# Moving the sums of squares of a linear-attention output, and of the compressed queries, by stages

## The chip, the cores and the metric

The kernel runs on one core of one Trainium2 chip. The metric is device time in microseconds (us). Three runs of the kernel before took 2260.86, 2266.12 and 2268.09 us, so the median is 2266.12 us.

## What is computed

The reference is a three-layer model on 1024 tokens of width 1024. The first layer mixes a convolution, a pooling branch and a differential attention, and ends in a mixture of 16 experts. The change doesn't touch it. The other two layers (numbered 0 and 1 here) are of one form:

```
u = rmsnorm(h, ln_mix[i]) @ w_in[i]
(c_q, c_kv, k_rope, gate_a, gq, gk, gv, lr_f, lr_b, gate_g) = split_cols(u, IN_SPLITS)
y_mla = mla_branch(c_q, c_kv, k_rope, ...) * silu(gate_a)
y_gla = gla_branch(gq, gk, gv, lr_f, lr_b, ..., gla_out_norm[i]) * silu(gate_g)
h = h + concatenate([y_mla, y_gla]) @ w_out[i]
h = h + sigmoid(rmsnorm(h, ple_norm[i]) @ w_ple_gate[i]) * (p[i] @ w_ple_proj[i])
```

Two parts matter. The linear attention (gla_branch) has four heads. For each it computes, in chunks of 64 tokens and in both directions, o = intra-chunk part + (queries times a running state), then rmsnorm(o_forward + o_backward) over the head's 128 columns. The softmax attention (mla_branch) works on compressed queries c_q (384 columns) and compressed keys and values c_kv (256 columns): both are normalised by their root mean square, the queries and keys get a part that rope rotates, and scores, softmax and values follow. Dividing a row of queries by its root mean square is the same as scaling its scores, so the kernel multiplies the raw c_q by its weights and applies the factor 1/rms inside the softmax.

## The kernel before

All activations stand transposed (features on partitions, 1024 tokens along the free axis). A float32 product is made of three matmuls on a high and a low half of each operand: helper split (line 451 makes the high half on ScalarE, line 447 the low half on VectorE, or, every third time, on GpSimd). In the code the engines are nc.tensor (PE), nc.vector (DVE), nc.scalar (ACT), nc.gpsimd (POOL) and nc.sync (SP).

The order of the work is written by hand with Python generators. Each yield ends a stage. `_weave(main, side, steps)` takes a stage of main, then on average `steps` stages of side, and so on; `_chain` runs generators one after the other. The framework that compiles the program takes this order as a priority: an instruction that it expects to be late can be overtaken by others of its engine. It fixes one order per engine, and each engine then runs its list strictly in that order. Buffers come from pools by tag: PSUM has four product buffers of 512 columns (tag mm: psT, psSq and others) and two of 1024 columns (tag sc: psGt, psA, psK, psDS, psO, psS, psKR and the scores). A buffer is taken when its tile is first written and is free after its last reader.

`second_layer` (line 2001) weaves two things after the first eight half products of gla_v. The main side is a chain of products from the input projection (mmT and gla_v: a stage is half a product of 512 columns, 12 matmuls of 128x512; psT or psV). The other side is `gla_heads(i, 16)` (line 1735), which starts one of four `gla_head` generators every 16 of its stages and advances all that are alive, oldest first. The stages of one head (line 1623), counted from 0, before the change:

- 0: psGt, the gate's product (L1633), its read-out; 2 and 3: scans and exponentials; 4 and 5: scaling of queries qd and keys kd; 6: two more scalings (POOL writes L, L1666)
- 8 and 9: psA, intra-chunk products (L1678), each read by a masked copy into xbuf (L1679), then summed on POOL (L1682)
- 10: psK, transposes (L1689); 11: two memsets; 12: psDS, state increments (L1700), two buffers of tag sc
- 13 to 15: the state chain st, 30 small VectorE instructions (L1703, L1706)
- 18: psO, the output (L1717 and L1720, 8 x 6 matmul records of 128 and 64 columns), copied to go by ACT (L1722)
- 19: ms_split: psS is taken, ACT squares go (L589), the square is split (sqh, sql); 21: psS, a product with ones in four matmuls (L595: two on sqh, two on sql), which sums over partitions
- 22: gr = 1/rms by ACT's Ln (L598) and Exp (L599); 23: go times weight times gr on DVE (L1727), times the gate on POOL (L1730), store by SP (L1732)

Inside the chain, c_q's three products (mla_c, line 1745) are woven at 0.5 with `mla_norm` (line 1776), which takes another buffer of tag sc for the sums of squares of c_kv (psS at L1786, read by ACT at L1788), while heads 2 and 3 are alive. mla_c also adds up the squares of c_q in one tile css.

After the heads come the rope inputs (mla_rope_in, four stages of 9 matmuls), and then a weave of `mla_nope` (line 1833: eight query stages of 9 matmuls and eight key stages of 6; ACT reads each into a high half, qnh or knh, L1823, and DVE makes the low half, qnl or knl, L1824) with a chain of `rope` (line 1860) and `mla_factor` (line 1799), at 1.2. Rope has 15 stages: 1 loads tables (SP), 2 multiplies the key part, 6 takes psKR and splits it, 7 and 8 multiply on POOL, 9 to 12 rotate the queries on DVE (L1892 to L1898), 13 splits their first half into r1h and r1l, 14 the second into r2h and r2l, and 15 issues 16 SP copies into qr (L1907). mla_factor is a single stage: eight one-column products psSq of css with ones (L1805), each seen as two matmul records, then rq by ACT (L1809, L1810) and DVE (L1812). rq scales the softmax. The scores (L460, psS<-krh,qr among them) start next; each takes three matmuls on qn and kn and two on qr.

Of the kernel before, what the change touches and what calls it, by code (L numbers as in the profile page):

```python
# [19 lines left out]
NT = 8  # L20
# [242 lines left out]
def _weave(main, side, steps=1.0):  # L263

    due = 0.0
    for _ in main:
        yield
        due += steps
        while due >= 1.0:
            due -= 1.0  # L270
            if next(side, _END) is not _END:
                yield
    yield from side
# [10 lines left out]
def _chain(*gens):  # L284
    for g in gens:
        yield from g
# [31 lines left out]
class _Kernel:  # L318
# [261 lines left out]
        nc.scalar.activation(out, ps, AF.Ln, bias=self.eps, scale=1.0 / n)  # L580
        nc.scalar.activation(out, out, AF.Exp, scale=-0.5)

    def ms_split(self, srcs, n, out):

        nc = self.nc
        ps = self.sc("psS")
        for j, s in enumerate(srcs):
            q = self.d("sqs")
            nc.scalar.activation(q, s, AF.Square)  # L589
            parts = self.split(q, "sq")  # L590
            yield
            yield
            for m, part in enumerate(parts):
                for b in (slice(0, 512), slice(512, 1024)):
                    nc.tensor.matmul(ps[:, b], self.ones_r, part[:, b], start=j == 0 and m == 0,  # L595
                                     stop=j == len(srcs) - 1 and m == 1)
            yield
        nc.scalar.activation(out, ps, AF.Ln, bias=self.eps, scale=1.0 / n)  # L598
        nc.scalar.activation(out, out, AF.Exp, scale=-0.5)  # L599
# [1023 lines left out]
    def gla_head(self, i, h):  # L1623
# [48 lines left out]
        for q in range(2):  # L1672
            ps = self.sc("psA", (128, 2, 4, 128))
            for a in range(4):
                for dr in range(2):
                    r = slice(64 * dr, 64 * dr + 64)
# [20 lines left out]
        for t in range(8):  # L1697
            for e in range(2):
                r = slice(64 * e, 64 * e + 64)
                nc.tensor.matmul(ds[e][:, t], kn[r, t], v(t)[r], start=True, stop=True)  # L1700
        yield
        for c in range(15):
            nc.vector.scalar_tensor_tensor(st[(c + 1) // 8][0:64, (c + 1) % 8], st[c // 8][0:64, c % 8],  # L1703
                                           er[0:64, 1, c:c + 1], ds[c % 2][0:64, c // 2], op0=OP.mult, op1=OP.add)
            r = 15 - c
# [4 lines left out]
        yield  # L1710
        yield
        yield

        o = self.d("go")
        ps = self.sc("psO", (128, 8, 128))
# [6 lines left out]
        nc.scalar.activation(o, ps.rearrange("p a b -> p (a b)"), AF.Copy)  # L1722
        yield
        r = self.d("gr")
        yield from self.ms_split([o], 128, r)
        yield
        nc.vector.scalar_tensor_tensor(o, o, self.col(("go", i)), r, op0=OP.mult, op1=OP.mult)  # L1727
        while h not in self.sg:
# [70 lines left out]
    def mla_factor(self, i):  # L1799

        nc = self.nc
        css = self.css.pop("cq")
        pc = self.mm("psSq", (128, 8))
        for t in range(NT):
            nc.tensor.matmul(pc[:, t:t + 1], css[:, 128 * t:128 * t + 128], self.ones[:, 0:1],  # L1805
                             start=True, stop=True)
        rq = self.const.tile([128, 2, 8], F32, name="rq", tag="rq")
        self.rq = rq[:, 0], rq[:, 1]
        nc.scalar.activation(rq[:, 1], pc, AF.Ln, bias=self.eps, scale=1.0 / 384)  # L1809
        nc.scalar.activation(rq[:, 1], rq[:, 1], AF.Exp, scale=-0.5)  # L1810
        for n, f in enumerate((192.0 ** -0.5, -192.0 ** -0.5)):
            nc.vector.tensor_scalar(rq[:, n], rq[:, 1], f, None, op0=OP.mult)  # L1812
        yield
# [187 lines left out]
    def second_layer(self, i, lead):  # L2001
# [4 lines left out]
        heads = self.gla_heads(i, 16)  # L2006
# [4 lines left out]
            values, self.gla_gate(i, 1), self.gla_qk(i, 2), self.gla_qk(i, 3),  # L2011
            self.gla_gate(i, 2), self.gla_gate(i, 3), self.mla_gate(i, 0), self.mla_gate(i, 1), self.mla_c(i, "ckv"),
            _weave(self.mla_c(i, "cq"), self.mla_norm(i), 0.5), self.mla_gate(i, 2), self.mla_gate(i, 3)),
            heads, 1.06)
        self.hm = None
        self.ahead = 1
        yield from self.mla_rope_in(i)
        yield from _weave(self.mla_nope(i), _chain(self.rope(i), self.mla_factor(i)), 1.2)
        self.ahead = 0
        attention = self.mla_attention(i)  # L2020
        values = self.mla_values(i)
# [271 lines left out]
```

## Time and profile before

| what | value |
|---|---|
| median of three runs | 2266.12 us |
| the profiled execution | 2267.0 us |
| its span in the profile | 2265.2 us |
| PE busy | 2142.4 us (95%) |
| DVE, ACT, POOL busy | 66%, 51%, 22% |
| TensorE's granted clock, mean over the span | 0.978 |

The profile's times are microseconds from the start of the span. "Busy" adds up the engine's instructions; a matmul's end is modelled, and consecutive matmuls overlap. A wait is idle time of an engine just before an instruction, put down to the instruction that released it. The granted clock is a share of TensorE's full speed: 1.00 is 2.4 GHz, 0.50 is 1.2 GHz, and a value between them is a mean over a stretch with both. In a timeline line, the first number is the start, the second the duration of the group of like instructions, "x" counts them, and the square bracket holds the idle time before the first, and its releaser. PEld is the weight load of a matmul.

### The profile page before, as it was taken

Reading aid. Unit: us, or ns where it says so; the run is one execution under the profiler, and the core shown is the slowest. Engines: PE = TensorE matmul, PEld = TensorE weight load, DVE = VectorE, ACT = ScalarE, POOL = GpSimd, SP = SyncE. Lnnn points to the kernel's source line nnn. Section 1 sums busy time; section 2 is a strip of 40 time slices with the busy share of each in tenths; the row PEclk is TensorE's granted clock in tenths of the full one; section 3 lists DMA queues with packets and bytes.
Section 4 is the critical chain, followed back from the end, with each engine's and each line's share of the span. In section 5 each row is a group of like instructions: output and inputs, shape, how many; then the busy total and the mean of one; then the engine's idle time right before and its main releaser. Section 6 shows DMA issues by size and latency. Waiting matters only on the chain.

```text
span 2265.2 us, 31258 instructions
## 1 busy us (share of the span) xinstructions
PE 2142.4 (95%) x11660; PEld 1814.3 (80%) x11660; DVE 1498.1 (66%) x2598; ACT 1153.1 (51%) x2192; POOL 493.8 (22%) x431
## 2 busy tenths in 40 slices
PE   7989888998999989999999999999999989999998
PEld 7878777787887778877788988888877777898886
DVE  5995788577788732677746674566367675675455
ACT  5314778435677654354444553456344444554344
POOL 1320144202232101112322331101011232332100
PEclk9999999999999999999999999999999999999999
DMA  5101231638999861011112024543001113013343
GB/s 199 47 19 57 75 84 34 213 118 290 282 326 325 268 235 56 28 38 66 45 58 56 10 75 160 187 144 129 10 28 57 47 66 84 11 43 135 121 149 130
DMA packets 78447, 255.09 MB, mean 113 GB/s; under 512 B 9680, under 2 KB 16976, under 8 KB 78288
## 3 DMA queue, kind: packets, MB, share of 16 engines
q1 hardware_dynamic: 65024, 205.84, 26.1%
q0 software_dynamic: 10672, 38.00, 7.1%
q10 hardware_dynamic: 2592, 9.18, 1.1%
q8 instruction: 94, 1.54, 0.3%
q14 instruction: 65, 0.53, 0.1%
HBM read 183.51 MB, written 58.98 MB: 107 GB/s over the span
## 4 chain that ended last, share of the span: by engine, by line
PE 46%; DVE 10%; issue 3%; ACT 3%; DMA 1%; POOL 1%; SPq 0%; DVEq 0%; ACTq 0%; POOLq 0%
PE psR L501 14%; PE psT L470 11%; PE psS L460 6%; PE psO L460 4%; PE psV L501 4%; PE psPT L1951 2%; DVE st L1703 2%; DVE st L1706 2%; PE psMV L460 1%; PE psX L550 1%; DVE wl L447 1%; PE psA L1678 1%; DVE B L1648 1%; PE psO L1720 1%; DVE B L1647 1%
## 5 line engine op out<-in xcount | busy, mean ns | idle before, releaser
L470 PE MATMUL psT<-mh,wh 128*128 128x512 f32 (+1 forms) x784 | 293.4, 375 | 9.9 <-ACT k L1569 4.3
L470 PE MATMUL psT<-ml,wh 128*128 128x512 f32 (+1 forms) x784 | 287.4, 367 | 2.1 <-DVE ml L559 2.1
L470 PE MATMUL psT<-mh,wl 128*128 128x512 f32 (+1 forms) x784 | 288.2, 368 | 0.0
L447 DVE TENSOR_TENSOR wl<-raw,wh 128x1024 fp32r<-128x1024 f32 x171 | 218.4, 1283 | 62.5 <-ACT wh L451 56.6
L451 ACT ACTIVATE wh<-raw 128x1024 fp32r<-128x1024 f32 x205 | 214.8, 1056 | 58.0 <-DMA raw<-in_wm_dram 25.0
L470 PEld LDWEIGHTS psT<-mh,wh 128*128 128x128 f32 x784 | 153.1, 195 | 36.9 <-ACT k L1569 5.0
L447 POOL TENSOR_TENSOR wl<-raw,wh 128x1024 fp32r<-128x1024 f32 x34 | 89.0, 2618 | 428.8 <-ACT wh L451 364.5
L470 PEld LDWEIGHTS psT<-ml,wh 128*128 128x128 f32 x784 | 153.2, 195 | 24.7 <-DVE ml L559 2.7
L470 PEld LDWEIGHTS psT<-mh,wl 128*128 128x128 f32 x784 | 152.5, 195 | 23.6
L501 PE MATMUL psR<-wh,mixh 128*128 128x512 f32 x384 | 152.3, 397 | 2.6 <-DVE mpT L1956 1.7
L501 PE MATMUL psR<-wh,mixl 128*128 128x512 f32 x384 | 149.9, 390 | 0.9 <-POOL mixl L447 0.9
L501 PE MATMUL psR<-wl,mixh 128*128 128x512 f32 x384 | 150.0, 391 | 0.0
L1939 POOL TENSOR_SCALAR mp<-mp,mrr 128x512 f32<-128x512 f32 x128 | 92.1, 731 | 213.6 <-DVE mrr L1937 209.9
L1935 ACT ACTIVATE mp<-psS,mnm,rq 128x1024 f32<-128x1024 f32 x64 | 77.4, 1209 | 82.9 <-DVE mnm L1932 82.9
L501 PE MATMUL psR<-wl,mh 128*128 128x512 f32 (+1 forms) x264 | 101.3, 384 | 1.2 <-DVE wl L447 1.2
L501 PE MATMUL psR<-wh,mh 128*128 128x512 f32 (+1 forms) x264 | 102.0, 386 | 0.0
L501 PE MATMUL psR<-wh,ml 128*128 128x512 f32 (+1 forms) x264 | 101.0, 383 | 0.0
L558 ACT ACTIVATE mh<-psX 128x256 fp32r<-128x256 f32 (+1 forms) x144 | 60.8, 452 | 78.1 <-PE psX L550 73.0
L460 PEld LDWEIGHTS psO<-mpT,mv 128*128 128x128 f32 x768 | 96.4, 191 | 2.6
L1930 DVE TENSOR_REDUCE mmx<-psS 128x1 f32<-128x1024 f32 x64 | 78.1, 1220 | 29.4 <-PE psS L460 29.3
L460 PE MATMUL psO<-mpT,mv 128*128 128x256 f32 x768 | 97.1, 283 | 0.0
L988 DVE TENSOR_TENSOR xr<-psR,xr 128x512 f32<-128x512 f32 x48 | 33.1, 691 | 94.1 <-PE psR L501 84.7
(490 smaller groups left out, 5691.5 us busy)
## 6 DMA issues: line engine op xcount, KB each, us to landing
raw<-in_wg_dram SPq DMA_DIRECT2D x109, 512.0 KB, 3.7
raw<-in_wm_dram SPq DMA_DIRECT2D x96, 512.0 KB, 6.8
pp<-ppo ACTq DMA_DIRECT2D x16, 512.0 KB, 5.8
h<-xr SPq DMA_DIRECT2D x16, 512.0 KB, 2.9
xr<-h SPq DMA_DIRECT2D x16, 512.0 KB, 4.8
ppr<-pp SPq DMA_DIRECT2D x16, 512.0 KB, 5.6
xt<-in_x_dram SPq DMA_DIRECT2D x8, 512.0 KB, 5.5
xr<-in_x_dram SPq DMA_DIRECT2D x8, 512.0 KB, 4.7
```

The source lines that it names most:

```text
L447: e.tensor_tensor(out, full, high.bitcast(F32), op=OP.subtract)
L451: self.nc.scalar.activation(h, src, AF.Copy)
L460: self.nc.tensor.matmul(out, a, b, start=j == 0, stop=j == n - 1)
L470: self.nc.tensor.matmul(ps, p[:, a], q, start=k == 0 and j == 0, stop=k == nk - 1 and j == 2)
L501: self.nc.tensor.matmul(out, p, q[:, b], start=k == 0 and j == 0, stop=k == 7 and j == 2)
L558: nc.scalar.activation(h, v, AF.Copy)
L1703: nc.vector.scalar_tensor_tensor(st[(c + 1) // 8][0:64, (c + 1) % 8], st[c // 8][0:64, c % 8], er[0:64, 1, c:c + 1], ds[c % 2][0:64, c // ...
L1706: nc.vector.scalar_tensor_tensor(st[(r - 1) // 8][64:128, (r - 1) % 8], st[r // 8][64:128, r % 8], er[64:128, 1, r:r + 1], ds[r % 2][64:12 ...
L1930: nc.vector.tensor_reduce(mx, ps, axis=AX.X, op=OP.max)
L1935: nc.scalar.activation(p, ps, AF.Exp, bias=nm, scale=self.rq[0][:, t:t + 1], accum_out=sm)
L1939: nc.gpsimd.tensor_scalar(p[:, b], p[:, b], rr, 1.0, op0=OP.mult, op1=OP.mult)
L1951: nc.tensor.transpose(pt[:, a, 128 * n:128 * n + 128], p[:, 256 * c + 128 * a:256 * c + 128 * a + 128], self.ident)
```

## The change

Four places. psO comes one stage later in each head (stage 19). ms_split takes a parameter, and a head calls it with three stages between split and product instead of two (split at 20, psS at 23, gr at 24, go at 25). mla_factor yields between its eight products. The two weaves get new rates: 1.09 for the heads; and mla_nope is woven at 1.6 with a weave of mla_factor and rope, two rope stages to one of mla_factor, instead of rope and then mla_factor. No instruction is added or removed.

```diff
--- before.py
+++ after.py
@@ -580,7 +580,7 @@
         nc.scalar.activation(out, ps, AF.Ln, bias=self.eps, scale=1.0 / n)
         nc.scalar.activation(out, out, AF.Exp, scale=-0.5)
 
-    def ms_split(self, srcs, n, out):
+    def ms_split(self, srcs, n, out, later=2):
 
         nc = self.nc
         ps = self.sc("psS")
@@ -588,8 +588,8 @@
             q = self.d("sqs")
             nc.scalar.activation(q, s, AF.Square)
             parts = self.split(q, "sq")
-            yield
-            yield
+            for _ in range(later):
+                yield
             for m, part in enumerate(parts):
                 for b in (slice(0, 512), slice(512, 1024)):
                     nc.tensor.matmul(ps[:, b], self.ones_r, part[:, b], start=j == 0 and m == 0,
@@ -1710,6 +1710,7 @@
         yield
         yield
         yield
+        yield
 
         o = self.d("go")
         ps = self.sc("psO", (128, 8, 128))
@@ -1722,7 +1723,7 @@
         nc.scalar.activation(o, ps.rearrange("p a b -> p (a b)"), AF.Copy)
         yield
         r = self.d("gr")
-        yield from self.ms_split([o], 128, r)
+        yield from self.ms_split([o], 128, r, 3)
         yield
         nc.vector.scalar_tensor_tensor(o, o, self.col(("go", i)), r, op0=OP.mult, op1=OP.mult)
         while h not in self.sg:
@@ -1804,6 +1805,8 @@
         for t in range(NT):
             nc.tensor.matmul(pc[:, t:t + 1], css[:, 128 * t:128 * t + 128], self.ones[:, 0:1],
                              start=True, stop=True)
+            if t < NT - 1:
+                yield
         rq = self.const.tile([128, 2, 8], F32, name="rq", tag="rq")
         self.rq = rq[:, 0], rq[:, 1]
         nc.scalar.activation(rq[:, 1], pc, AF.Ln, bias=self.eps, scale=1.0 / 384)
@@ -2011,11 +2014,11 @@
             values, self.gla_gate(i, 1), self.gla_qk(i, 2), self.gla_qk(i, 3),
             self.gla_gate(i, 2), self.gla_gate(i, 3), self.mla_gate(i, 0), self.mla_gate(i, 1), self.mla_c(i, "ckv"),
             _weave(self.mla_c(i, "cq"), self.mla_norm(i), 0.5), self.mla_gate(i, 2), self.mla_gate(i, 3)),
-            heads, 1.06)
+            heads, 1.09)
         self.hm = None
         self.ahead = 1
         yield from self.mla_rope_in(i)
-        yield from _weave(self.mla_nope(i), _chain(self.rope(i), self.mla_factor(i)), 1.2)
+        yield from _weave(self.mla_nope(i), _weave(self.mla_factor(i), self.rope(i), 2.0), 1.6)
         self.ahead = 0
         attention = self.mla_attention(i)
         values = self.mla_values(i)
```

## Rows read from the trace of the kernel before

**Rows 1.** Page, part 1, PE: busy us, share of the span, instructions.

```profile
PE 2142.4 (95%) x11660; PEld 1814.3 (80%) x11660; DVE 1498.1 (66%) x2598; ACT 1153.1 (51%) x2192; POOL 493.8 (22%) x431
```

**Rows 2.** Windows: length, busy PE, PEld, DVE, ACT, POOL, granted clock, DMA share, GB/s.

```profile
933.00:1150.00 217.00, 205.32 (x1146) 170.12 (x1144) 148.35 (x272) 102.29 (x150) 51.02 (x27) 0.96 0.14 49
```

**Rows 3.** PE's waits: line <- releaser: total us, times, longest.

```profile
PE psGt L1633 <- DVE st L1703: 8.6, 4, 2.9
...
PE psS L595 <- DVE sql L447: 7.2, 4, 2.4
...
PE psO L1717 <- DVE st L1703: 3.4, 2, 1.7
...
PE psS L595 <- POOL sql L447: 3.1, 2, 1.6
...
PE psA L1678 <- ACT gr L598: 2.5, 1, 2.5
...
PE psS L460 <- DMA qr<-r2l: 0.9, 1, 0.9
```

**Rows 4.** Timeline of PE, layer 1, head 1: the two halves of psS.

```profile
1754.56 0.72 PE L595 MATMUL psS<-sqh,ones 128*128 128x512 f32 x2
...
1758.65 0.73 PE L595 MATMUL psS<-sql,ones 128*128 128x512 f32 x2 [2.44 <-DVE sql L447]
```

**Rows 5.** Windows as in rows 2: psO and what follows, both layers; around psS.

```profile
1128.60:1138.50 9.90, 9.85 (x48) 9.85 (x49) 3.33 (x5) 1.95 (x3) 0.00 (x0) 0.53 0.30 100
1849.50:1855.00 5.50, 5.46 (x49) 5.46 (x49) 3.31 (x5) 1.95 (x3) 0.00 (x0) 1.00 0.53 176
1138.50:1148.90 10.40, 10.40 (x39) 8.38 (x39) 3.03 (x4) 5.92 (x7) 2.40 (x1) 0.79 0.10 35
1855.00:1863.30 8.30, 8.30 (x39) 6.86 (x39) 3.98 (x3) 5.64 (x7) 2.40 (x1) 1.00 0.10 35
1683.70:1692.00 8.30, 8.30 (x38) 6.87 (x38) 7.28 (x15) 6.10 (x11) 0.58 (x1) 1.00 0.00 0
1695.40:1705.30 9.90, 9.90 (x37) 7.71 (x35) 3.54 (x5) 4.45 (x6) 3.48 (x2) 0.83 0.16 55
```

**Rows 6.** Timelines of PE and ACT, head 2's psS to head 3's psK.

```profile
1096.09 0.72 PE L595 MATMUL psS<-sql,ones 128*128 128x512 f32 x2 [1.14 <-DVE sql L447]
1106.39 0.87 PE L1689 MATMUL psK<-sq,B 128*128 128x128 f32 x6 [1.43 <-DVE xbuf L1679]
...
1100.74 1.12 ACT L598 ACTIVATE gr<-psS,sm 128x1024 f32<-128x1024 f32 x1 [2.18 <-PE psT L470]
...
1813.81 0.73 PE L595 MATMUL psS<-sql,ones 128*128 128x512 f32 x2 [1.44 <-POOL sql L447]
...
1821.61 1.11 ACT L598 ACTIVATE gr<-psS,sm 128x1024 f32<-128x1024 f32 x1
...
1822.77 3.38 PE L1678 MATMUL psA<-qd,kd 64*128 64x128 f32 x32 [2.54 <-ACT gr L598]
```

**Rows 7.** Layer 0: the query sums on PE; the window behind them.

```profile
1191.33 1.95 PE L1805 MATMUL psSq<-ones,css 128*128 128x1 f32 x16
...
1193.60:1198.00 4.40, 4.37 (x12) 3.46 (x13) 3.71 (x7) 2.72 (x5) 0.00 (x0) 0.61 0.42 99
```

**Rows 8.** DVE and ACT timelines at rope's end, both layers; landing of qr's copies.

```profile
1193.46 0.68 DVE L1824 TENSOR_TENSOR knl<-psT,knh 128x512 fp32r<-128x512 f32 x1
1194.80 1.23 DVE L447 TENSOR_TENSOR r2l<-qx,r2h 128x1024 fp32r<-128x1024 f32 x1 [0.66 <-ACT r2h L451]
...
1905.42 1.22 DVE L1898 TENSOR_TENSOR qx<-qx,ro 128x1024 f32<-128x1024 f32 x1
...
1907.54 0.27 ACT L1809 ACTIVATE rq<-psSq,sm 128x8 f32<-128x8 f32 x1 [3.22 <-PE psSq L1805]
...
1907.95 1.04 ACT L451 ACTIVATE r2h<-qx 128x1024 fp32r<-128x1024 f32 x1
...
DMA to landing us min/median/max: 2.2/2.3/3.9
```

## The prediction

> **What bounds the kernel now.** I read the page first: TensorE (PE) is busy 95% of the span [rows 1]. So an edit that moves work without removing any can gain only where PE stands still or runs slow. The windows by stage come next: while the linear-attention heads run (933 to 1150 us in layer 0, 217 us), PE is busy 205.3 us, 11.7 less than the stretch, and its granted clock averages 0.96, where 1.00 is the 2.4 GHz level and 0.50 the 1.2 GHz one [rows 2]. Layer 1 repeats it. Then PE's waits over the whole kernel, kept to the lines that the diff moves [rows 3]: the sum-of-squares product psS waits for the low half of its split operand (sql) 7.2 + 3.1 = 10.3 us in six places; psO waits for the state chain st 3.4 us in two, 1.7 each; psGt of the next head waits for st 8.6 us in four; psA once 2.5 us for gr; the first scores 0.9 us for qr. Last I read windows around single places for the clock [rows 5].
>
> **The sum, part by part.** It starts from the profiled execution, 2267.0 us (span 2265.2), 0.9 above the median of the runs shown, 2266.1. The source yields stages; I counted by hand between which half products (12 matmuls) each stage falls. 36 psT matmuls fill the stretch 1855.0 to 1863.3, so a stage of 12 is 8.3 / 3 = 2.8 us [rows 5].
>
> (a) psS three stages after its split instead of two. From psO to psS there were 36, 24, 12 and 36 matmuls for heads 0 to 3; after, I count 48, 36, 36 and 48, so 2.8 us more to cover the waits. Those seen are at most 2.4 [rows 3]; the largest stands in layer 1, where psS on sqh came first, some psT matmuls were put between, and PE then stood 2.44 us [rows 4]. But that also shows that the order on PE isn't the source's: the planner had pulled matmuls forward, and with sql expected sooner it will pull fewer. I leave 1 us in two places: 10.3 - 2.3 = 8.0 us gained. Bounds: half of it (5), all of it (10.3).
>
> (b) The slow stretch behind one of these waits. After the 2.2 us wait in layer 1, 36 psT matmuls took 9.9 us at granted clock 0.83, against 8.3 us at 1.00 before it [rows 5]. That is 1.6; I take 1.5 as gone. Bounds 0 and 1.6.
>
> (c) psO a stage later. Heads 0 to 2 don't wait there. Head 3 waits 1.7 us in each layer [rows 3]. Its psDS, too, comes 12 to 24 matmuls earlier, since the weave runs at 1.09, and its psK and psDS crowd onto one stage: counted, psDS to psO goes from 60 to 60 to 72 matmuls. Half of 3.4: 1.7 gained. Bounds 0 and 3.4.
>
> (d) The slow stretch at that wait in layer 0: psO took 9.9 us at clock 0.53, against 5.5 at 1.00 in layer 1; the 36 psT behind it 10.4 against 8.3 [rows 5]. Together 6.5 us. The same 1.7 us wait in layer 1 left the clock at full, so this is chance; I count half, 3.3. Bounds 0 and 6.5.
> [...]
>
> (e) The norm that psA now meets. gr frees the PSUM buffer that psS holds, one of two of the tag; it comes in the very stage in which the next head's psA starts, where two or three stages lay between. For heads 0 and 1 the other buffer is free, and I cost it at nothing: psA's second half has one stage, 2.8 us, of cover. For head 2 the second buffer belongs to the norm of the compressed keys, emitted in the same stage. There gr's Ln ended 1821.61 + 1.11 - 1814.54 = 8.2 us after psS in layer 1, and 1100.74 + 1.12 - 1096.81 = 5.1 in layer 0 [rows 6]; with one stage of products between, PE would stand 5.4 and 2.3, 7.7 together. Today it stands 2.54 before psA and 1.43 before psK there [rows 6], 4.0. I take half the difference, a loss of 2. Bounds: -4 (waits gone) and +4, plus what rival D adds. Behind gr go DVE's and POOL's products of go, and SP's store of it, two stages later; POOL's now lies between the two xsum, whose second only psO needs, ten stages on. Free while psO isn't early.
>
> (f) The weave at 1.09. 75 side stages instead of 73 against 69 main ones, so the heads end where they did. psDS to the next psGt keeps its 48, 48 and 36 matmuls, so the 8.6 us for st stay. Nothing; bounds -2 and +2.
>
> (g) The sums for the queries. Today 16 one-column matmuls stand together, 1.95 us; 12 products after that ran at 0.61 [rows 7]. Spread, the matmuls cost the same PE time. What ends last there is not PE, though: the scores wait for qr, by DMA (2.2 us or more) from the last split of rope [rows 8]; so neither the slow products nor the gap gives time back. What counts is when r2l comes. Rope now advances 1.6 x 2/3 = 1.07 steps per product instead of 1.2, which puts r2l behind two more knl on a busy DVE: 2 x 0.68 = 1.4 us later [rows 8]. Against that, ACT no longer stands 3.22 us in front of psSq before it can split r2h, and DVE's 0.66 us wait for r2h goes [rows 8]. Net 1.4 - 0.7 = +0.7 us in layer 0; about 0 in layer 1, where r2l is on POOL and r2h, ready at the end of the last rotation, 1906.64, started at 1907.95 [rows 8]. psSq also keeps one of four product buffers until rq; PE has to wait for knl sooner, but before scores that wait anyhow. PE, done sooner, then stands longer before qr, and a slow clock can fall onto the scores; the price is the 12 products' excess, 4.4 - 2.8 = 1.6 us [rows 5, 7], in one layer of two: +1.6. Total +2.3. Rope's table loads on SP come a product later, with nothing behind them but rope. Bounds: -2 and +9 (in both layers two more products of 1.4 us, if PE sets the pace, and the slow stretch).
>
> Sum: -8.0 - 1.5 - 1.7 - 3.3 + 2 + 2.3 = -10.2, so 2267.0 - 10.2 = **2256.8**.
>
> **Rivals.**
> A is the forecast, 2256.8; its own range is 2246 to 2260.
> E, everything covered: (a) to (d) at their upper bounds, 21.8, with (e) and (g) at zero: 2245. For it speaks that a stage, 2.8, exceeds each wait; against it, that the planner refills gaps.
> B, the waits move: VectorE is busy 148.4 of 217 us in the heads' stretch [rows 2], and PE, running ahead, meets st or gr instead. Only 5 of (a) and nothing of (b) to (d), less (g): 2267.0 - 5 + 2.3 = 2264.3.
> C, the slow stretches don't follow these waits: thin products such as psO cause them, and as many come back elsewhere. Then (b) and (d) give nothing: 2256.8 + 4.8 = 2261.6. For it: one 1.7 us wait with and one without a slow stretch [rows 3, 5]. Against it: the fall to 0.83 in the products right behind a wait [rows 5].
> [...]
> D, slower: the PSUM buffer that psS holds. If the planner gives psA that buffer, or ACT is late with gr everywhere as it is at head 2, three places in each layer wait. It decides once the six cost over (10.2 + 2) / 6 = 2.0 us each. Priced: head 2's 7.7 - 4.0 = 3.7, the four others 2.3 each (9.2), and a slow stretch of 1.6 at each of the six (9.6): 22.5 in place of the 2 in the sum, 2277.3. For it: ACT's lag of 5.1 and 8.2 [rows 6]; against it: one wait of 2.5 for gr so far [rows 3].
> That the batch stays together is also possible, since the planner reorders; by (g) it would change little.
>
> **How the numbers follow.** A 0.53, E 0.09, B 0.17, C 0.12, D 0.09. A measurement of this kernel tells about 0.3%, 6.8 us, from no change: faster is below 2259.3, slower above 2272.9. Faster: A but for 0.04, E, and 0.02 of C: 0.60. Same: 0.04 of A, 0.10 of C, B: 0.31. Slower: D, 0.09. For 8 in 10 the range leaves out D and half of E: 2245 to 2267.
>
> **What would show it.** Right: psS waiting under 3 us for sql over all heads; psO without wait at head 3; the full clock through psO in layer 0; one-column matmuls in eight pairs among the products; qr still the last release before the scores. Wrong: PE waits for gr before psA at heads 1 to 3 above 2 us each; the scores' wait for qr above 4 us; the heads' stretch not shorter than 217 us by at least 5.

## The result and the profile after

The changed kernel took 2279.32 us (median of six runs, 2276.58 to 2285.62), the kernel before 2266.14 on the same chip. The ratio is 1.0064, with a 95% interval of 1.0042 to 1.0086: slower by 0.4 to 0.9%. The forecast was 2256.8. The profiled execution took 2281.57 us, its span 2279.8. The page's first part, PE, with the columns of [rows 1]:

```profile
PE 2140.4 (94%) x11660; PEld 1811.7 (79%) x11660; DVE 1502.4 (66%) x2598; ACT 1154.5 (51%) x2192; POOL 499.1 (22%) x431
```

The instructions are the same in number, and PE is busy 2 us less than before; so the time is in PE's idle. To find it I cut both traces at the same events: a layer's first gv product, its first product of the rope inputs, its last score. That makes a "heads" and a "tail" stretch for each layer. Windows of the kernel before (columns as in [rows 2]): heads and tail of layer 0, then of layer 1.

```profile
886.64:1155.21 268.57, 256.89 (x1372) 212.74 (x1371) 167.64 (x301) 120.07 (x178) 54.47 (x29) 0.97 0.12 42
1155.21:1346.61 191.40, 190.10 (x1103) 165.52 (x1102) 131.19 (x220) 101.04 (x183) 60.69 (x74) 0.99 0.16 45
1600.70:1869.62 268.92, 253.90 (x1374) 209.40 (x1372) 173.23 (x301) 119.21 (x178) 54.16 (x29) 0.98 0.12 42
1869.62:2061.90 192.28, 190.48 (x1104) 165.34 (x1102) 128.35 (x220) 101.14 (x183) 62.42 (x74) 0.99 0.15 45
```

The same four windows of the changed kernel:

```profile
890.89:1161.16 270.27, 259.04 (x1372) 214.50 (x1371) 172.68 (x301) 120.37 (x178) 57.84 (x29) 0.96 0.12 42
1161.16:1356.49 195.33, 190.19 (x1103) 165.44 (x1102) 131.09 (x220) 101.14 (x183) 60.66 (x74) 0.99 0.15 44
1608.89:1875.82 266.93, 253.51 (x1374) 209.84 (x1372) 171.21 (x301) 120.44 (x178) 56.59 (x29) 0.98 0.12 42
1875.82:2076.51 200.69, 193.09 (x1104) 167.05 (x1103) 130.40 (x220) 101.28 (x183) 62.66 (x74) 0.97 0.15 43
```

The heads took 537.5 us before and 537.2 after: nothing gained. The tails took 383.7 and 396.0: 12.3 lost. Length less PE busy is PE's idle time: in the heads it fell from 26.7 to 24.6 and PE busy rose by 1.8 (the same instructions at a lower clock); in the tails idle rose from 3.1 to 12.7 and busy by 2.7. The code up to 890.89 is unchanged; over the 14 profiles here it took between 885.2 and 892.5, so a single span carries some 7 us of chance, and only stretches are compared below.

PE's waits after, in the form of [rows 3]:

```profile
PE psGt L1633 <- DVE st L1703: 13.4, 6, 2.8
PE psS L460 <- DMA qr<-r2l: 8.4, 2, 5.0
...
PE psO L1718 <- DVE st L1703: 4.0, 2, 2.5
PE psK L1689 <- DVE xbuf L1679: 2.8, 2, 1.4
PE psS L595 <- POOL sql L447: 2.5, 2, 1.4
PE psKR L1884 <- DVE kx L1877: 2.4, 1, 2.4
```

The waits of psS for sql fell from 10.3 to 2.5, as the change intended, and psA's 2.5 for gr went. But psGt now waits 13.4 for st where it waited 8.6, psO 4.0 where it waited 3.4, and in the tail the scores wait 8.4 for qr where they waited 0.9, and psKR 2.4 for kx.

### The profile page after: what moved, and what is told of

It reads as the page before. It is cut to its first block, busy times and chain, and to the rows that moved or that the text cites. A ratio compares the mean times of both kernels' runs of the same rounds, so it can differ in the third digit from the quotient of the medians.

```text
span 2279.8 us, 31242 instructions
## 1 busy us (share of the span) xinstructions
PE 2140.4 (94%) x11660; PEld 1811.7 (79%) x11660; DVE 1502.4 (66%) x2598; ACT 1154.5 (51%) x2192; POOL 499.1 (22%) x431
```

## The experiments

Every ratio is against the kernel before, run beside it on the same chip. In the table, the heads and tail columns are lengths in us from each one's profile, cut as above (layer 0, layer 1).

| kernel | ratio, 95% interval | heads | tail |
|---|---|---|---|
| before | 1 | 268.6, 268.9 | 191.4, 192.3 |
| after | 1.0064 (1.0042 to 1.0086) | 270.3, 266.9 | 195.3, 200.7 |
| e1 heads' part alone | 0.9986 (0.9969 to 1.0003) | 270.5, 267.0 | 191.5, 192.5 |
| e2 tail's part alone | 1.0045 (1.0022 to 1.0068) | 261.9, 267.3 | 195.1, 200.8 |
| e3 sums spread, rope's pace near the old | 1.0009 (0.9990 to 1.0027) | 268.4, 271.0 | 192.0, 197.8 |
| e4 sums in one batch, rope's pace as after | 1.0016 (0.9996 to 1.0035) | 267.1, 269.2 | 196.7, 197.2 |
| e5 both later stages, weave at 1.06 | 0.9925 (0.9901 to 0.9949) | 258.2, 258.8 | 191.5, 194.1 |
| e6 only the product with ones later, 1.06 | 0.9965 (0.9937 to 0.9992) | 264.5, 267.9 | 191.6, 192.2 |
| e7 tail's part, rq scaled on ScalarE | 1.0041 (1.0019 to 1.0064) | 268.2, 271.0 | 195.2, 198.1 |
| e8 before with a faster rope | 1.0044 (1.0023 to 1.0064) | 262.0, 267.4 | 199.1, 200.0 |
| e9 whole change at 1.06 | 0.9971 (0.9953 to 0.9988) | 258.3, 258.8 | 195.4, 199.4 |
| e10 only psO later, 1.06 | 0.9967 (0.9947 to 0.9988) | 263.3, 264.9 | 191.2, 194.0 |
| e11 only the weave at 1.09 | 1.0061 (1.0041 to 1.0081) | 274.2, 273.1 | 191.5, 192.5 |
| e12 e5, sums in one batch ahead of rope | 0.9940 (0.9922 to 0.9958) | 258.1, 260.2 | 192.8, 196.3 |

**Which half of the change costs.** e1 keeps the heads' part and undoes the tail's; e2 the reverse.

e1, against the changed kernel:

```diff
-            if t < NT - 1:
-                yield
...
-        yield from _weave(self.mla_nope(i), _weave(self.mla_factor(i), self.rope(i), 2.0), 1.6)
+        yield from _weave(self.mla_nope(i), _chain(self.rope(i), self.mla_factor(i)), 1.2)
```

e2 is the same diff with the signs turned, against the kernel before.

> Only the heads' part of the change: psO a stage later, three stages between split and product, the heads' weave at 1.09; the query sums and rope as before. Theory T (the loss sits in the tail, in rope's pace): 2260 to 2269 us, no slower than before; PE's waits for sql fall under 4 us, those for the state chain (psGt, psO) rise from 12 to 16 us or more. Rival H (the heads' part is itself the loss): 2273 us or more.

> Only the tail's part: query sums spread, weave at 1.6 with two rope stages to one of the sums; the heads as before. Theory T: 2274 to 2281 us, the whole loss, with 6 to 9 us of waits for qr before the scores. Rival H: 2262 to 2269.

e1 came out at 0.9986, about nothing, and e2 at 1.0045, some 10 us. e2's two tails are the changed kernel's, 195.1 and 200.8; e1's are those of before. So the tail's part is a loss by itself, and the heads' part gives nothing to set against it. The two ratios add up to 1.0031, below the 1.0064 of both together, but within their intervals. In e2 the heads of layer 0, whose code is unchanged, took 261.9 instead of 268.6, because no slow stretch fell on psO of head 3 in that execution (5.6 us there, at 1.00): what the clock does there in one execution is chance.

**What in the heads' part took its gain back.** e5 adds both later stages at the old rate, 1.06. Against the kernel before (with ms_split's new parameter):

```diff
         yield
         yield
         yield
+        yield

         o = self.d("go")
...
-        yield from self.ms_split([o], 128, r)
+        yield from self.ms_split([o], 128, r, 3)
```

e6 has only the second of the two edits, e10 only the first. e11 changes the rate and adds no stage:

```diff
-            heads, 1.06)
+            heads, 1.09)
```

e9 is the whole change with this one line put back.

> The heads' part (psO a stage later, three stages between split and product) at the old weave rate of 1.06, tail as before. Theory T2 (1.09 draws the state increments psDS towards the end of a gate's VectorE work, so the state chain starts late and eats what the later psS gives): psGt's waits for st back to 8 to 10 us, psS's waits under 4, the two stretches of the heads together 5 to 9 us shorter than before, 2259 to 2264 us. Rival W (PE only runs ahead into st, whatever the rate): psGt's waits 12 us or more, 2265 to 2269.

> Only the three stages between split and product, at the old rate 1.06; psO where it was. T2: waits for sql under 4 us, psO's wait at head 3 as before (3.4 us), stretches of the heads 4 to 8 us shorter, 2260 to 2266. Rival W: no shorter.

> The whole change with one number undone: the heads' weave back at 1.06. Theory (the rate alone turns the heads' gain into new waits for st, and the tail costs some 12 us by itself): the heads' stages, from the first gv product to the first product of the rope inputs, take 258 to 262 us in each layer, as in the kernel with only the two later stages at 1.06 (258.2 and 258.8), psGt waits about 8.6 us for st, and the tail's 396 us stay; 2266.3 - 16.7 + 12 = about 2262, ratio 0.998. Rival (what the heads gain at 1.06 was the clock's chance, or the tail eats it): the heads' stages over 265 us and a ratio of 1.003 or more.

> Only psO a stage later, split and rates as before. Theory (the two later stages add up): with both 2249.7 and the later product with ones alone 2261.4, psO's share is about 11 us: 2255, ratio 0.995; the waits for sql stay at some 10 us, psO's for st fall from 3.4 to about 1, and psO in layer 0 runs at the full clock. Rival (psO's stage only helps where the product with ones comes later too): ratio 0.999 to 1.001, the heads' stages at 266 to 269 us.

> Only the heads' weave at 1.09, no stage added. Theory (the rate puts psDS one stage of products nearer to psK, behind a gate's VectorE work, so that st comes late): psK to psDS 12 instead of 24 matmuls at head 0, psGt's waits for st 12 to 14 us instead of 8.6, the waits for sql still about 10; 5 to 10 us slower than the kernel before, ratio 1.002 to 1.0045. Rival (it is the added stages at 1.09 that crowd it): psGt's waits 8 to 9 us, ratio 0.999 to 1.001.

The windows of the heads in e5, layer 0 and layer 1, and PE's waits there:

```profile
890.40:1148.62 258.22, 248.28 (x1373) 205.87 (x1372) 173.28 (x301) 119.65 (x178) 55.44 (x28) 1.00 0.13 43
...
1594.28:1853.12 258.84, 251.16 (x1374) 208.53 (x1373) 174.08 (x301) 119.51 (x178) 53.62 (x28) 0.99 0.13 43
```

```profile
PE psGt L1633 <- DVE st L1703: 8.6, 4, 2.9
...
PE psS L595 <- POOL sql L447: 2.1, 2, 1.4
PE psA L1678 <- ACT mr L1789: 1.8, 1, 1.8
PE psS L595 <- DVE sql L447: 1.6, 1, 1.6
...
PE psO L1718 <- DVE st L1703: 1.1, 1, 1.1
```

The heads are 20.4 us shorter than before, 10.3 and 10.1 in the two layers, where my expectation had 5 to 9 for both. PE's idle in them is 17.6 us instead of 26.7: psS waits 3.7 instead of 10.3, psO 1.1 instead of 3.4, and psGt's 8.6 has not grown. PE busy is 499.4 instead of 510.8, so 11.4 of the 20.4 is clock in this execution: it stands at 1.00 and 0.99 where it stood at 0.97 and 0.98. How much of that lasts is taken up at (b), (d) below. e6 and e10 show that the two stages each give about half, 0.9965 and 0.9967, and that these nearly add up to the 0.9925 of both.

Then the rate alone, e11: the windows of the heads, and PE's waits.

```profile
887.80:1162.00 274.20, 258.43 (x1372) 213.42 (x1371) 172.76 (x301) 119.23 (x178) 58.30 (x29) 0.96 0.13 43
1606.03:1879.13 273.10, 256.13 (x1373) 211.48 (x1372) 169.47 (x301) 118.73 (x178) 55.08 (x29) 0.98 0.12 43
```

```profile
PE psGt L1633 <- DVE st L1703: 11.6, 6, 2.8
...
PE psS L595 <- ACT sqh L451: 6.1, 4, 2.7
PE psS L595 <- POOL sql L447: 5.1, 2, 3.7
...
PE psO L1717 <- POOL cl L447: 3.1, 1, 3.1
PE psO L1717 <- DVE st L1703: 2.6, 1, 2.6
```

1.09 by itself costs 1.0061, 13 us: the heads are 9.8 longer, with idle of 32.7 instead of 26.7. My expectation had the sign and the place but not all of it: psGt's wait grew to 11.6, not 12 to 14, and the rest came at psS, which waits also for the high half of the square (6.1; 12.9 in all, against 10.3), and at psO (5.7 against 3.4). The stages that come sooner by the rate come sooner for every reader in the chain. Idle grew by 6 us; about as much is clock, which over all executions was lower in e11 than in the kernel before, as (b), (d) below show. e9 is the cross-check: with the rate back, the whole change is no longer slower but 0.9971, with e5's heads and the changed kernel's tails, at the 2262 that the theory gave to within 3 us (2259.2).

Where the rate bites first can be read from a timeline. The changed kernel, layer 0, head 0, PE and DVE (columns as explained for timelines above):

```profile
949.19 2.06 PE L1700 MATMUL psDS<-gv,kn 64*128 64x128 f32 x32
...
951.14 0.69 DVE L568 SCALAR_TENSOR_TENSOR sgg<-sgg,psT 128x512 f32<-128x512 f32 x1 [0.79 <-ACT sgg L567]
952.53 0.69 DVE L1587 TENSOR_TENSOR sgg<-sgg,psT 128x512 f32<-128x512 f32 x1 [0.70 <-ACT sgg L569]
953.13 0.33 DVE L1703 SCALAR_TENSOR_TENSOR st<-st,er,psDS 64x128 f32<-64x128 f32 x1
...
964.23 0.70 PE L1633 MATMUL psGt<-gk,gw 96*128 96x512 f32 x2 [1.87 <-DVE st L1703]
```

And e5, at the same place:

```profile
951.39 2.06 PE L1700 MATMUL psDS<-gv,kn 64*128 64x128 f32 x32
...
952.01 0.69 DVE L1587 TENSOR_TENSOR sgg<-sgg,psT 128x512 f32<-128x512 f32 x1 [0.70 <-ACT sgg L569]
953.48 0.34 DVE L1703 SCALAR_TENSOR_TENSOR st<-st,er,psDS 64x128 f32<-64x128 f32 x1 [0.78 <-PE psDS L1700]
...
964.57 0.70 PE L1633 MATMUL psGt<-gk,gw 96*128 96x512 f32 x2
```

In e5 the state chain waits for psDS. In the changed kernel, counted from the layer's first gv product (890.89, in e5 890.40), psDS comes 2.7 us sooner, one stage of products, but DVE's list holds a gate's three steps (sgg, two of them shown) ahead of st, each waiting for ScalarE. So st starts only 0.8 us sooner. psGt needs a buffer of tag sc, and both of these hold psDS until st has read them. PE has 48 matmuls between psDS and psGt in both kernels, gets to psGt 1.9 us too soon, and stands; e11 has the same wait there, 1.9. The other places at which the rate costs I have not traced one by one.

**What in the tail costs.** The change does two things there: the sums are spread, and rope advances more slowly. e3 spreads them at nearly the old pace of rope, e4 keeps the batch and takes the new pace, e7 leaves the tail's part as it is and moves two small instructions to another engine, e8 goes the other way and makes rope faster.

e3 has the change's yields in mla_factor, and

```diff
-        yield from _weave(self.mla_nope(i), _chain(self.rope(i), self.mla_factor(i)), 1.2)
+        yield from _weave(self.mla_nope(i), _weave(self.rope(i), self.mla_factor(i), 0.5), 1.8)
```

e4 and e8 change only a number of that line, the rate 1.2, to 1.0667 and to 1.6. e7, against e2:

```diff
-            nc.vector.tensor_scalar(rq[:, n], rq[:, 1], f, None, op0=OP.mult)
+            nc.scalar.activation(rq[:, n], rq[:, 1], AF.Copy, scale=f)
```

> Query sums spread as in the change, but rope keeps its old pace of 1.2 stages per product (sums woven at 0.5 into rope, the whole at 1.8); heads as before. Theory T (rope's pace): 2260 to 2270, waits for qr under 3 us. Rival S (it is the spreading, by the product buffer that is held over all products or by the matmuls between them): 2274 or more, like the tail alone.

> The suspected cost alone: query sums in one batch behind rope, as before, and rope slowed to 1.067 stages per product, its pace in the change; heads as before. Theory T: 2271 to 2280, waits for qr of 4 us or more in all. Rival S: 2263 to 2269, as before.

> The tail's part alone, with the two small scalings that finish rq done by ScalarE instead of VectorE. Theory P (in layer 1 these two, 128x8, took 1.7 and 2.3 us beside POOL's rope products, where 0.16 is usual, and pushed kx<-k,sin and psKR back): psKR's 2.4 us wait for kx in layer 1 goes, layer 1's tail (rope inputs to last scores) is 3 to 5 us shorter than with the tail alone, layer 0's stays within 1 us; 2271 to 2276. If it is rope's pace alone, both layers' tails stay as they are, 2276 to 2280.

> Dose of rope's pace the other way: rope, then the query sums in one batch, as before, but at 1.6 stages per product instead of 1.2; heads as before. Theory T (pace sets when qr lands): no wait for qr, the tails of both layers together 1 to 5 us shorter, 2262 to 2267. Rival: rope was not the last to arrive at the old pace, or the products then wait for VectorE: tails as before or longer by up to 3 us, 2266 to 2271.

Either of the two changes alone lengthens the tails, by 6.1 (e3) and 10.2 us (e4) against the 383.7 of before; in the ratios, 1.0009 and 1.0016, neither stands out from no change, so their shares are read from one profile each and are rough. Their sum is more than the 12.3 of both: they delay the same end, the landing of qr. By layer, the pace alone (e4) costs 5.3 and 4.9, the spreading alone (e3) 0.6 and 5.5: the pace costs in both layers, the spreading in layer 1. In e3, theory and rival both missed: 2272.8 us lies between them, and the waits for qr, 4.2 us, are over the theory's 3.

The pace: in layer 0 of the changed kernel DVE had 14 low halves (qnl, knl) ahead of r2l instead of 12. r2l ended 42.9 us after the rope inputs began, where it had ended at 40.8; the scores waited 3.45 for qr, where they had not waited (the 0.9 of before stood in layer 1).

The spreading: the changed kernel's timelines. First psSq in layer 0, then layer 1: POOL's products of rope, DVE's two scalings of rq (ns min/median/max, first and last start) and the key's second product, psKR and the first score.

```profile
1171.36 0.28 PE L1806 MATMUL psSq<-ones,css 128*128 128x1 f32 x2
1175.69 0.28 PE L1806 MATMUL psSq<-ones,css 128*128 128x1 f32 x2
1180.01 1.39 PE L1806 MATMUL psSq<-ones,css 128*128 128x1 f32 x12
1183.08 0.37 DVE L1815 TENSOR_SCALAR rq<-rq 128x8 f32<-128x8 f32 x2
...
1896.78 2.40 POOL L1891 TENSOR_TENSOR rt<-qx,sin 128x1024 f32<-128x1024 f32 x1
1899.13 2.38 POOL L1893 TENSOR_TENSOR ro<-qx,sin 128x1024 f32<-128x1024 f32 x1
...
L1815 DVE TENSOR_SCALAR rq<-rq x2: 1700/2004/2307, 1897.5 to 1899.2; 128x8 f32<-128x8 f32 x2
...
1902.16 1.22 DVE L1877 TENSOR_TENSOR kx<-k,sin 64x1024 f32<-64x1024 f32 x1
...
1903.44 3.34 PE L1884 MATMUL psKR<-kx,rot 128*128 128x512 f32 x4 [2.44 <-DVE kx L1877]
...
1925.36 0.76 PE L460 MATMUL psS<-krh,qr 128*128 128x512 f32 x1 [4.96 <-DMA qr<-r2l]
```

The source asks for eight separate sums over the query and key products. The order that came out has two, and then six together, all among the query products; layer 1 has the same. So rq is ready early and not late. Its two scalings of 128 x 8 elements took 0.37 us together in layer 0. In layer 1, beside POOL's rope products, they took 1.70 and 2.31, 4.04 from first to last: the first ended at 1899.20 and POOL's rt at 1899.18, the second at 1901.54 and ro at 1901.51. The key's product kx, behind them on DVE, came late, psKR waited 2.44 and then ran at a granted clock of 0.57 (3.34 us for four matmuls; in e7, behind a wait of 1.65, 1.98 us at 1.00), and everything that follows in rope came late: 4.96 us before the first score, and then a slow stretch on the scores:

```profile
1207.60:1211.00 3.40, 3.40 (x10) 2.62 (x9) 1.44 (x2) 0.53 (x1) 0.00 (x0) 0.50 0.88 199
1924.40:1931.20 6.80, 5.84 (x14) 4.61 (x15) 1.44 (x2) 0.91 (x1) 0.00 (x0) 0.50 0.89 201
```

e7 takes the two scalings off DVE. Its layer 1, DVE, POOL and PE:

```profile
1898.48 2.93 DVE L1876 TENSOR_TENSOR kx<-k,sin 64x1024 f32<-64x1024 f32 x1
...
1897.95 2.38 POOL L1892 TENSOR_TENSOR ro<-qx,sin 128x1024 f32<-128x1024 f32 x1
...
1901.47 1.98 PE L1883 MATMUL psKR<-kx,rot 128*128 128x512 f32 x4 [1.65 <-DVE kx L1876]
```

The tail of layer 1 is 2.7 us shorter than e2's, and psKR's wait 1.65 instead of 2.4; the total, 1.0041, hardly moved. The scalings gone, kx itself met POOL's ro and took 2.93 us instead of 1.22. So the scalings were one link and not the whole cause; with the pace as it is, rope's chain comes late in any case, as e4 shows.

e8 was the miss. With rope ahead at 1.6, qr should have been early and the tails shorter; PE does not wait for qr at all, and yet the tails are 15.4 us longer and the kernel is slower, 1.0044. The rival had the products wait for VectorE, but the tails at most 3 us longer. PE's waits in e8:

```profile
PE psSq L1805 <- DVE qnl L1824: 6.2, 2, 3.6
PE psT L470 <- DVE qnl L1824: 5.5, 2, 3.2
```

Now rope's rotations stand ahead of the low halves in DVE's list, and the products wait 11.7 us for qnl to free their PSUM buffers. Neither 1.07 nor 1.6 is as good as the old pace: DVE does both jobs, and the old 1.2 lies between the two losses; no pace in between was run with rope first.

**A version that beats both.** e5 does: 2249.66 us against 2266.33, ratio 0.9925 (0.9901 to 0.9949). I also tried to better its tail, with the sums in one batch ahead of rope, where nothing can be in their way. e12, against e5:

```diff
-        yield from _weave(self.mla_nope(i), _chain(self.rope(i), self.mla_factor(i)), 1.2)
+        yield from _weave(self.mla_nope(i), _chain(self.mla_factor(i), self.rope(i)), 1.3)
```

> The two later stages at 1.06, and the query sums in one batch ahead of rope instead of behind it, rope at 1.3. Theory (the tail is set by when r2l comes; ScalarE stood 3.2 us in front of psSq before it could split the second half, and with the sums in front it does not): the tail's two layers take 380 to 384 us against 385.5 in the kernel with the heads' part alone, about 2247 to 2250, ratio 0.992. Rival (the two scalings of rq on VectorE come beside GpSimd's rope products again and push the key part): a wait of psKR for kx of 1 us or more, the tail 388 us or more, ratio 0.994 or more.

2251.39 us, ratio 0.9940 (0.9922 to 0.9958): the tails are 389.1 instead of e5's 385.5. The rival's size came true but not its mechanism: psKR waits only 0.5 for kx; rope starts a step later, r2l with it, and the scores wait 4.5 us for qr. e5 stands.

## Why the prediction was wrong, point by point

(a) "I leave 1 us in two places: 10.3 - 2.3 = 8.0 us gained." The waits for sql did fall, by 7.8, to 2.5. At the old rate (e5) they fall by 6.6. The step held; what it left out is (f). I had also not looked at why the waits were so long. In the kernel before, three of the five splits that VectorE makes took 2.92 us and not 1.22, beside GpSimd's product L (the five in ns, min/median/max; then layer 1, head 1):

```profile
L447 DVE TENSOR_TENSOR sql<-sqs,sqh x5: 1222/2922/2926, 976.7 to 1755.7; 128x1024 fp32r<-128x1024 f32 x5
...
1755.67 2.93 DVE L447 TENSOR_TENSOR sql<-sqs,sqh 128x1024 fp32r<-128x1024 f32 x1
...
1755.21 2.30 POOL L1666 TENSOR_TENSOR L<-qd,er 128x1024 f32<-128x1024 f32 x1 [9.50 <-ACT er L1659]
```

psS waited 1.4, 2.2 and 2.4 us for these three, 6.1 of the 10.3. With psO a stage later (e5, e10) no split on VectorE meets L, and their median is 1.23; in e6, where psO stays, the three still take 2.93, and the longer way to psS covers all but 1.0 us of it.

(b), (d) The slow stretches. In the changed kernel the clock did not come back. The window of psO at head 3 of layer 0, which answers to the 0.53 in [rows 5]:

```profile
1131.50:1142.50 11.00, 10.58 (x50) 10.49 (x51) 5.08 (x7) 2.96 (x5) 1.49 (x1) 0.55 0.30 98
```

It runs at 0.55, behind a wait of 2.5 for st. At 1.06 the heads' PE busy fell by 11.4 us, more than the 4.8 that I took and more than the 8.1 of my upper bounds, since other slow stretches behind waits went too. How much of that lasts can't be told from one profile: without any change to the heads they were 8.1 us less busy in e2's and 9.3 in e8's. The mean granted clock over all executions says more. It was 0.9835 in e5, where the kernel before, run beside it, had 0.9819; 0.9851 against 0.9822 in e10, 0.9816 against 0.9819 in e6 and 0.9790 against 0.9822 in e11. Length times (1 - clock) is an estimate of what the clock costs; for psO in [rows 5] it gives 9.9 x 0.47 = 4.7 us, where 4.4 were lost. By it e5 won some 4 us and e10 7, e6 none, and e11 lost 7. So clock came back with psO's later stage, about as much as (b) and (d) took, and the new rate cost it again.
The Trainium skill, "TensorE: Matmul & The Clock Gate", section "Loop structure matters more than you think", has VectorE copy a result out between tiles without breaking the array's warmth, where the next matmuls follow at once. In this trace they did not follow at once: PE stood 2.5 us for VectorE, and the thin products behind that ran at 0.55. In e5, layer 0, psGt waited 2.9 us for VectorE and the whole stretch stood at 1.00. So such a wait can go with a loss of clock, and need not.

(c) "Half of 3.4: 1.7 gained." psO waited 4.0, not 1.7; e5 shows 1.1 and e10 none, so the added stage does what was said, and the rate undid it: between psDS and psO of head 3 stand 59 matmuls, with 60 to 72 counted and 72 in e5.

(e) "a loss of 2". There was no wait for gr in the changed kernel. The 4.1 us that PE stood before psA and psK turned into 2.8 before psK and 1.4 before psDS, so nothing changed in sum. That is within the bounds; rival D, which was built on gr, did not come. That its 2277.3 lies near the measured 2279.3 is luck.

(f) This is the step that failed in the heads: "75 side stages instead of 73 against 69 main ones, so the heads end where they did. psDS to the next psGt keeps its 48, 48 and 36 matmuls, so the 8.6 us for st stay. Nothing; bounds -2 and +2." The matmul counts held, nearly (48, 53 and 42 came out, 48, 50 and 42 before). What was wrong was to take the matmuls behind psDS as the cover of st. st begins when DVE reaches it, and DVE was held by the gate's steps; at head 0, where I traced it, psDS came 2.7 us sooner and st 0.8. Measured by itself (e11), the rate costs 13 us, over six times the bound: 6 of it idle, the rest about what the clock lost. Rival B named the mechanism, PE running ahead of VectorE and meeting st, but put no wait on the rate and stopped at 2264.3.

(g) The term that was mis-sized: "Total +2.3 ... Bounds: -2 and +9". It measured +12.3 in the profile and about +10 by e2's ratio. The pace was right in kind: r2l moved by 2.1 us in layer 0, where I had 0.7 net. Layer 1, put at "about 0", was the larger loss, 8.4: the pace alone costs 4.9 there (e4), the spreading alone 5.5 (e3). That "spread, the matmuls cost the same PE time" was true and beside the point: the spread moved rq forward to where GpSimd worked, which I hadn't looked at, since I had counted eight pairs evenly and the order gave two and a batch. The 1.6 for a slow stretch on the scores came in both layers.

**The sum.** My steps (a) to (e) made -12.5 us, and the runs with these stages alone give -16.7. Add +13 for the rate and +10 for the tail, both measured by themselves, and the change comes to some +7; measured, +13. The intervals of the three cover the difference. But the whole change against e9 sets the rate at 21 us, where e11 sets it at 13; whether rate and tail make each other worse is not shown. The forecast had the parts that gain, and put +2.3 on the two that lose.

**By the signs I had set.** Right: psS waits under 3 us for sql (2.5); qr is the last release before the scores. Wrong: psO waits at head 3 in both layers, and at 0.55 in layer 0; the sums are not eight pairs; one of the two waits for qr is over 4 us (5.0); the heads are not 5 us shorter. Of the waits for gr nothing came.

## What to carry to other kernels

Where two streams are woven, a new rate moves every stage of the side stream, also those that were in order; test it apart from the edit that it comes with, and add stages at the old rate first. Matmuls counted between producer and reader are cover only if the engine between starts when the producer ends: read what stands ahead of it in that engine's list, and what that waits for. Where one engine serves two chains, as in this tail, putting either of them first can move the wait to the other's reader.

## What the runs showed of the hardware

Two VectorE instructions on 128 x 8 elements took 0.37 us together, and 4.04 beside two GpSimd products of 2.4 us, each ending with one of these; a 64 x 1024 product of two operands took 2.93 instead of 1.22 beside the same GpSimd work (e7). This and the split of 2.93 us shown above each ended 1.08 us after GpSimd's instruction. That fits the Trainium skill, "SBUF — State Buffer", section "🔬 SBUF: two separate sides", by which GpSimd and VectorE, with two operands in SBUF or in a two-port mode, share a port pair that one of them holds for a whole instruction while the other stands still. In which mode the scalings, with one such operand, ran is not shown. What I had not expected is that the size of the instruction doesn't protect it: 0.16 us became 1.7 and 2.3.

The clock's share is uneven: in one execution of each, 11.4 of the 20.4 us that e5 gains in the heads are the same instructions at a higher clock, where the mean clock of all executions gives some 4 us (estimated above); and unchanged heads of layer 0 took 261.9, 262.0 and 267.1 to 268.6 us in different executions.
